# Two-layer hybrid scan and MLP backbone: modulation matmuls in halves of eight, their raw tiles in the ring of the weight halves, and the scan-state update as a sum and a scaling

## The chip, the core and the metric

The kernel runs on one core of a Trainium2 chip. The metric is the device time of one execution in microseconds (us). Inputs and result are fp32: a dense product is made of three single-pass products of split operands, the small products of the scans run in fp32 or, inside a triangular inverse, in fp16.

## The reference, cut to what matters

Two layers over 512 latent and 256 context tokens of width 1024. Each layer has a token mixer (a projection to 44 tiles of 128 columns, four pairs of RWKV-7 heads and two pairs of GLA heads that scan the tokens in both directions, gates, an output projection) and an MLP. Both are modulated by a product of the conditioning vectors with `ada_w`:

```python
mod_lat = (jax.nn.silu(c) @ ada_w[l] + ada_b[l])[:, None, :]
mod_ctx = jax.nn.silu(c_ctx) @ ada_w[l] + ada_b[l]
...
s = s * w_t - (s . kk_t) (kk_t * a_t) + v_t k_t      # RWKV-7 state, per token
...
s_next = s * dec + kv                                 # GLA state, per chunk of 64
```

The kernel computes both scans by chunks of 64 tokens: within a chunk everything is matrix products, and between chunks a state of 64 rows per head is carried on by a multiplication with the chunk's decay E and an addition of what the chunk brings.

## The kernel before, in words

**Stages.** A head part (load, first norm, first third of the modulation), then `mixer(0)`, `out_mlp(0)`, `mixer(1)`, `out_mlp(1)` (L1935 to L2003). In a mixer, 18 units follow each other: four RWKV pairs and two GLA pairs, three groups of 256 tokens each. `rw_C` (L1324) is the serial part of an RWKV unit: four steps `st`, each with both directions `d` and both heads `h` of a pair. A step goes through the engines in this order: TensorE makes `pp` from the state `zs` (in the profile `c<-ZS,AR`), ScalarE and VectorE each copy half of it to `pre`, TensorE makes `pq` (`c<-pre,YI`), both copy it to `za` (`ZA<-c`), TensorE makes `pr` (`c<-ZA,TK`), and the next state is written (`ZS<-c,E,zse`). Before, that last part is two operations: ScalarE scales the old state by E into `zse` (four instructions of 64x64), and VectorE multiplies `pr` by E and adds `zse` (four `scalar_tensor_tensor`). `gla_C` (L1579) does the same with `ze` and `GZ` and instructions of 64x128.

**What lies around the scans.** The dense products of the projections and of the gates (`d<-sh,wh`, `d<-sl,wh`, `d<-sh,wl`) are poured between the scan steps. `ada_steps` (L746) computes the remaining five sixths of the modulation: 5 blocks of 32 steps, each step one DMA of a raw tile `wa` (256 KB), four matmuls with 32 columns of weights (`da<-wa,SC`; the array is used as four column groups), and one addition of 128x128 to `acc` on VectorE; at the end of a block `acc` is transposed by four matmuls with the identity (`da<-C,acc`). The same way of transposing, `mm(..., ident)`, stands in `rstd_b` (L808, `d<-C,sc`) and in `sum_sq` (L815, `d<-C,rn`). Transposes of the scan operands are `pe.transpose` already (`m<-C,BK`).

**Buffers.** A dense weight tile comes in two halves. `load_w` (L674) loads each into a raw tile `wr0` or `wr1` (2 buffers each), ScalarE rounds it to `wh`, and VectorE or GpSimd subtracts to get `wl`. In a mixer the gates and every second output tile use `wr1`, the other projections `wr0`. The raw modulation tile `wa` has a buffer of its own (1).

**Order.** All instructions are recorded by a planner, the class `Order` (L151), and issued in the order of its list schedule, one flush per stage (five). It groups neighbouring matmuls of one kind (L277), gives each node a cost, and picks per engine the earliest ready node; among equals the one due first. `SEG` (L142) holds its settings per stage: HYST is a penalty for a node that changes the shape of TensorE's array, LATE and LATEF delay dense products and gate products against their due time, WARM says from what activity on it prefers dense products, AHEAD and HOLD bound how early DMAs are issued. `CFG` (L102) says how many gate tiles (`nfill`) and modulation steps (`nada`) are recorded with each unit. TensorE, ScalarE, VectorE, GpSimd and the DMA queue of SyncE each work strictly in the issued order. Line 566, where the nodes are issued, is the line of nearly every instruction of the profile, so rows are told apart by their tiles.

Of the kernel before, what the change touches and what calls it, by code (L numbers as in the profile page):

```python
# [53 lines left out]
def constants():  # L54
# [45 lines left out]
SB = 6  # L100

CFG = {  # L102
    "nfill": ((2, 2, 0, 3, 1, 0, 3, 1, 0, 2, 2, 0, 2, 1, 1, 0, 0, 0, 0), (2, 3, 0, 2, 2, 1, 2, 2, 0, 2, 0, 0, 2, 1, 1, 0, 0, 0, 0)),
    "nada": ((2, 2, 2, 2, 2, 2, 2, 2, 2, 1, 2, 2, 0, 1, 0, 0, 0, 0, 0), (2, 1, 3, 1, 3, 2, 3, 1, 0, 0, 0, 0, 0, 0, 0, 0, 0, 0, 0)),
# [38 lines left out]
    dict(AHEAD=20.0, HOLD=8000.0, HYST=0.0, LATE=80000.0, LATEF=80000.0, SLACK=0.0, WARM=0.45),  # L143
    dict(AHEAD=100.0, HOLD=1000000000.0, HYST=0.0, LATE=20000.0, LATEF=20000.0, SLACK=0.0, WARM=0.45),
    dict(AHEAD=20.0, HOLD=1000000000.0, HYST=0.0, LATE=20000.0, LATEF=20000.0, SLACK=0.0, WARM=0.45),
    dict(AHEAD=20.0, HOLD=8000.0, HYST=0.0, LATE=20000.0, LATEF=20000.0, SLACK=0.0, WARM=0.45),
    dict(AHEAD=20.0, HOLD=1000000000.0, HYST=0.0, LATE=20000.0, LATEF=20000.0, SLACK=0.0, WARM=0.6),
# [3 lines left out]
class Order:  # L151
# [57 lines left out]
    def add(self, key, op, fn, a, k):  # L209
# [36 lines left out]
        else:  # L246
            c = max(w(out), max([w(x) for x in ins if x.ap and len(x.ap) > 1], default=0))
            onchip = [x for x in ins if hasattr(x.tensor, "cap_key")]
            if key == "ACT":
                n["d"] = 175.0 + 0.87 * c + (100.0 if any(isinstance(k.get(x), bass.AP) for x in ("bias", "scale")) and c > 64 else 0.0)  # L250
                n["table"] = 1 if k.get("func") == AF.Ln else 0 if k.get("func") in (AF.Exp, AF.Tanh) else None
            elif key == "POOL":
# [4 lines left out]
                elif k.get("op") == ALU.pow:  # L257
                    n["d"] = 380.0 + 160.0 * c
                else:
                    n["d"] = 185.0 + 2.16 * c  # L260
                n["two"] = op == "tensor_tensor"
            else:
# [6 lines left out]
                else:  # L269
                    n["d"] = 150.0 + 1.05 * c  # L270
        if key == "PE":
# [5 lines left out]
            if GROUP and p is not None and p.get("kind") == n["kind"] and p["calls"] < (3 if lhs.dtype == F32R else 4 if n["dense"] else 16):  # L277
# [51 lines left out]
    def flush(self):  # L329
# [6 lines left out]
        for n in ns:  # L336
# [6 lines left out]
            for name, t in ts.items():  # L343
                left[name] = left.get(name, 0) + 1
                if name not in self.serial:
                    key = t.cap_key
                    kk = self.slots.setdefault(key, {"cap": t.bufs or t.tag_meta.bufs, "free": [], "used": 0, "next": {}, "n": {}, "t0": self.free0})
                    sub = "da" if name.startswith("da_") else ""
# [225 lines left out]
def hybrid_kernel(ctx: ExitStack, tc: tile.TileContext, A: dict, out: bass.AP):  # L574
# [171 lines left out]
    def ada_steps(l, b0, pl, tag, bufs):  # L746
        acc = prm.tile([P, 512], F32, name="acc", tag="acc", bufs=1)
        for k in range(KT):
            for u in range(4):
                raw = pl.tile([P, 4, 128], F32, name="wa", tag=tag, bufs=bufs)  # L750
                sp.dma_start(out=raw, in_=A["ada"][l, b0 // 2, k, u].rearrange("p (g m) -> p g m", g=4))
                ps = ips.tile([P, 512], F32, name="da", tag="i")[:, 0:128]
                for g in range(4):
                    mm(ps[32 * g:32 * g + 32, :], SC[:, k, :], raw[:, g])
# [1320 lines left out]
```

## Time and profile before

| | us |
|---|---|
| median of 3 runs | 2871.23 |
| lowest, highest | 2870.66, 2878.29 |
| the profiled execution | 2886.5 |
| its span, first to last instruction | 2884.7 |

| engine | busy us | share of the span |
|---|---|---|
| TensorE, matmuls (PE) | 2714.0 | 94% |
| TensorE, weight loads (PEld) | 2249.0 | 78% |
| VectorE (DVE) | 1603.8 | 56% |
| ScalarE (ACT) | 1470.5 | 51% |
| GpSimd (POOL) | 1172.0 | 41% |

Matmuls overlap each other, so the time that one costs is read from start to start, and a busy share of PE near 100% still hides short gaps. An fp32 matmul has two records, a single-pass one and a transpose have one. The granted clock is a mean over a stretch of TensorE's two levels, 2.4 GHz (1.00) and 1.2 GHz (0.50).

### The profile page before, as it was taken

Reading aid. Unit: us, or ns where it says so; the run is one execution under the profiler, and the core shown is the slowest. Engines: PE = TensorE matmul, PEld = TensorE weight load, DVE = VectorE, ACT = ScalarE, POOL = GpSimd, SP = SyncE. Lnnn points to the kernel's source line nnn. Section 1 sums busy time; section 2 is a strip of 40 time slices with the busy share of each in tenths; the row PEclk is TensorE's granted clock in tenths of the full one; section 3 lists DMA queues with packets and bytes.
Section 4 is the critical chain, followed back from the end, with each engine's and each line's share of the span. In section 5 each row is a group of like instructions: output and inputs, shape, how many; then the busy total and the mean of one; then the engine's idle time right before and its main releaser. Section 6 shows DMA issues by size and latency. Waiting matters only on the chain.

```text
span 2884.7 us, 57083 instructions
## 1 busy us (share of the span) xinstructions
PE 2714.0 (94%) x22596; PEld 2249.0 (78%) x22596; DVE 1603.8 (56%) x3154; ACT 1470.5 (51%) x3144; POOL 1172.0 (41%) x1336
## 2 busy tenths in 40 slices
PE   7999999999989989999999899989988988999998
PEld 6777877788767878888888666767776766888887
DVE  6677787775576351122224547787877677622224
ACT  4565655666773452313134545656566785633333
POOL 3653444443321642313135546434434232733335
PEclk9999999999999999999998999999988999999999
DMA  6322333222226322222223342223211125433334
GB/s 232 110 85 73 97 95 97 84 90 65 87 94 229 94 77 63 64 64 64 63 70 116 119 143 87 77 85 90 92 34 35 34 77 182 136 106 97 97 95 136
DMA packets 148444, 276.59 MB, mean 96 GB/s; under 512 B 16496, under 2 KB 25456, under 8 KB 148176
## 3 DMA queue, kind: packets, MB, share of 16 engines
q1 hardware_dynamic: 148176, 272.93, 30.4%
q8 instruction: 178, 2.92, 0.4%
q14 instruction: 90, 0.74, 0.1%
HBM read 242.85 MB, written 30.02 MB: 95 GB/s over the span
## 4 chain that ended last, share of the span: by engine, by line
PE 51%; DVE 7%; ACT 4%; POOL 4%; issue 2%; DMA 1%; SPq 0%; POOLq 0%; ACTq 0%; DVEq 0%
PE d L566 43%; PE c L566 3%; PE m L566 2%; PE i L566 2%; POOL wl L566 1%; POOL S L566 1%; POOL x L566 1%; DVE sl L566 1%; DVE ZS L566 1%; DVE AR L566 1%; DVE u L566 1%; ACT zse L566 1%; PE da L566 1%; DVE GZ L566 0%; ACT f L566 0%
## 5 line engine op out<-in xcount | busy, mean ns | idle before, releaser
L566 PE MATMUL d<-sh,wh 128*128 128x512 f32 (+1 forms) x3280 | 1199.2, 366 | 39.0 <-ACT sh L566 13.2
L566 PE MATMUL d<-sh,wl 128*128 128x512 f32 (+1 forms) x3280 | 1142.4, 348 | 19.1 <-POOL wl L566 16.4
L566 PE MATMUL d<-sl,wh 128*128 128x512 f32 (+1 forms) x3280 | 1142.1, 348 | 4.4 <-DVE sl L566 3.0
L566 POOL TENSOR_TENSOR wl<-wr,wh 128x512 fp32r<-128x512 f32 x356 | 476.0, 1339 | 793.9 <-ACT wh L566 770.6
L566 PEld LDWEIGHTS d<-sh,wh 128*128 128x128 f32 x3280 | 631.3, 192 | 150.0 <-issue 36.5
L566 PEld LDWEIGHTS d<-sh,wl 128*128 128x128 f32 x3280 | 631.0, 192 | 103.8 <-POOL wl L566 21.9
L566 PEld LDWEIGHTS d<-sl,wh 128*128 128x128 f32 x3280 | 632.7, 193 | 69.0 <-DVE sl L566 5.4
L566 ACT ACTIVATE wh<-wr 128x512 fp32r<-128x512 f32 x580 | 361.9, 627 | 469.3 <-PE d L566 389.6
L566 DVE TENSOR_TENSOR wl<-wr,wh 128x512 fp32r<-128x512 f32 x224 | 171.5, 770 | 187.0 <-ACT wh L566 178.9
L566 DVE TENSOR_TENSOR t<-t,d 128x512 f32<-128x512 f32 (+1 forms) x101 | 58.2, 576 | 318.2 <-ACT t L566 318.1
L566 POOL TENSOR_TENSOR sl<-t,sh 128x512 fp32r<-128x512 f32 (+2 forms) x72 | 103.3, 1435 | 204.8 <-ACT sh L566 204.7
L566 DVE TENSOR_TENSOR a<-a,d 128x512 f32<-128x512 f32 (+1 forms) x80 | 44.3, 554 | 232.7 <-PE d L566 232.7
L566 ACT ACTIVATE zse<-ZS,E 64x64 f32<-64x64 f32 x352 | 121.3, 345 | 67.2 <-DVE ZS L566 62.7
L566 ACT ACTIVATE XY<-i 128x512 f16<-128x512 f32 x192 | 107.8, 591 | 59.1 <-PE i L566 57.1
L566 ACT ACTIVATE t<-d 128x512 f32<-128x512 f32 (+1 forms) x101 | 51.4, 509 | 161.4 <-PE d L566 161.3
L566 DVE SCALAR_TENSOR_TENSOR ZS<-c,E,zse 64x64 f32<-64x64 f32 x352 | 99.5, 283 | 34.6 <-PE c L566 27.6
L566 POOL TENSOR_TENSOR LTL<-AB,LTB 64x512 f16<-64x512 f32 x48 | 63.9, 1332 | 122.1 <-DVE LTB L566 88.1
L566 POOL TENSOR_TENSOR rn<-rn,C 128x2 f32<-128x2 f32 (+2 forms) x41 | 59.3, 1446 | 101.4 <-DVE rn L566 94.9
L566 POOL TENSOR_TENSOR S<-S,q 128x256 f32<-128x256 f32 x92 | 76.5, 838 | 56.5 <-ACT q L566 52.8
L566 PEld LDWEIGHTS <-XY 64*64 64x64 f16 x1920 | 65.7, 110 | 38.9 <-issue 27.2
L566 DVE TENSOR_TENSOR Q<-i,MK 128x512 f16<-128x512 f32 x120 | 82.7, 689 | 23.3 <-PE i L566 20.7
L566 ACT ACTIVATE f<-d 128x512 f32<-128x512 f32 (+1 forms) x85 | 54.0, 644 | 79.1 <-PE d L566 69.2
(255 smaller groups left out, 4309.6 us busy)
## 6 DMA issues: line engine op xcount, KB each, us to landing
wr<-in_w_dram SPq DMA_DIRECT2D x304, 256.0 KB, 2.6
wr<-in_win_dram SPq DMA_DIRECT2D x180, 256.0 KB, 2.9
wa<-in_ada_dram SPq DMA_DIRECT2D x160, 256.0 KB, 2.7
wr<-in_wmrg_dram SPq DMA_DIRECT2D x64, 256.0 KB, 2.9
ra<-in_ada_dram SPq DMA_DIRECT2D x32, 256.0 KB, 5.4
wr<-in_wout_dram SPq DMA_DIRECT2D x32, 256.0 KB, 3.0
gdr<-fg SPq DMA_DIRECT2D x20, 384.0 KB, 2.9
gdr<-fg SPq DMA_DIRECT2D x20, 256.0 KB, 2.3
```

The lines of the kernel that those rows point to most:

```text
L566: ins = fn(*a, **k).ins
```

## The change

1. **Modulation in halves.** A step of `ada_steps` takes two raw tiles, issues eight matmuls into 128x256 of PSUM and adds 128x256 to `acc`: 16 steps a block in place of 32. The planner may group 8 such matmuls (before: 4).
2. **Raw tiles in the ring `wr1`.** `wa` has no buffer of its own any more; it shares `wr1`, which gets 3 buffers (before: 2, and 1 for `wa`).
3. **Transposes.** `mm(..., ident)` becomes `pe.transpose(..., ident)` at four places: 88 calls in `rstd_b`, 42 in `sum_sq`, 24 at the ends of the modulation blocks.
4. **Update as sum and scaling.** No `zse` and no `ze`. In layer one (`ACCUM[0]` is False) VectorE adds `pr` and the old state into `gs`, then multiplies by E: two instructions for each of two heads, both directions in one. In layer two (`ACCUM[1]`) TensorE adds the old state in PSUM by a matmul with the identity ahead of the one with `tk`, and VectorE multiplies by E: one instruction for each head. `gla_C` adds and multiplies on VectorE in both layers.
5. **Planner.** Some costs, the settings of all five stages and the tables `nfill` and `nada`.

```diff
+ACCUM = (False, True)
...
-    dict(AHEAD=20.0, HOLD=8000.0, HYST=0.0, LATE=80000.0, LATEF=80000.0, SLACK=0.0, WARM=0.45),
-    dict(AHEAD=100.0, HOLD=1000000000.0, HYST=0.0, LATE=20000.0, LATEF=20000.0, SLACK=0.0, WARM=0.45),
...
-    dict(AHEAD=20.0, HOLD=8000.0, HYST=0.0, LATE=20000.0, LATEF=20000.0, SLACK=0.0, WARM=0.45),
...
+    dict(AHEAD=20.0, HOLD=8000.0, HYST=2000.0, LATE=80000.0, LATEF=80000.0, SLACK=0.0, WARM=0.42),
+    dict(AHEAD=20.0, HOLD=1000000000.0, HYST=2000.0, LATE=20000.0, LATEF=20000.0, SLACK=0.0, WARM=0.4),
...
+    dict(AHEAD=400.0, HOLD=1000000000.0, HYST=0.0, LATE=20000.0, LATEF=0.0, SLACK=0.0, WARM=0.3),
...
-            raw = wp.tile([P, 4, 128], F32, name="wr", tag=f"wr{i}", bufs=2)
+            raw = wp.tile([P, 4, 128], F32, name="wr", tag=f"wr{i}", bufs=2 + i)
...
-                for g in range(4):
-                    mm(ps[32 * g:32 * g + 32, :], SC[:, k, :], raw[:, g])
-                au = acc[:, 128 * u:128 * u + 128]
+                for v in range(2):
+                    for g in range(4):
+                        mm(ps[32 * g:32 * g + 32, 128 * v:128 * v + 128], SC[:, k, :], raws[v][:, g])
+                au = acc[:, 256 * u:256 * u + 256]
...
-            mm(pt[:, s].rearrange("p g r -> p (g r)"), acc[:, 128 * s:128 * s + 128], ident)
+            pe.transpose(pt[:, s].rearrange("p g r -> p (g r)"), acc[:, 128 * s:128 * s + 128], ident)
...
-                if not (gi == NG - 1 and st == 3):
-                    zse = G([P, 2, 64], "zse", 1)
-                    for d in range(2):
-                        for h in range(2):
-                            act.activation(out=zse[HS[h], d], in_=zs[HS[h], cc[d], h, :], func=AF.Copy, scale=E[HS[h], cc[d]:cc[d] + 1])
...
                 for d in range(2):
-                    mm(fl(pr[:, d]), tk[:, cc[d]], fl(za[:, cc[d]]))
-                for d in range(2):
-                    for h in range(2):
-                        hs = HS[h]
-                        dve.scalar_tensor_tensor(out=nz[hs, ns[d], h, :], in0=pr[hs, d, h], scalar=E[hs, cc[d]:cc[d] + 1],
-                                                 in1=zse[hs, d], op0=ALU.mult, op1=ALU.add)
+                    if ACCUM[l]:
+                        mm(fl(pr[:, d]), ident, fl(zs[:, cc[d]]), stop=False)
+                    mm(fl(pr[:, d]), tk[:, cc[d]], fl(za[:, cc[d]]), start=not ACCUM[l])
+                for h in range(2):
+                    hs = HS[h]
+                    src = pr[hs, :, h]
+                    if not ACCUM[l]:
+                        src = G([P, 2, 64], "gs", 1)[hs]
+                        dve.tensor_tensor(out=src, in0=pr[hs, :, h], in1=zs[hs, sl, h, :], op=ALU.add)
+                    dve.tensor_tensor(out=nz[hs, ns, h, :], in0=src, in1=E[hs, sl].unsqueeze(2).to_broadcast([64, 2, 64]), op=ALU.mult)
...
-            g = ada_steps(l, b0, wp, "wa", 1)
-            r += [("a", g)] * (4 * KT)
+            g = ada_steps(l, b0, wp, "wr1", 3)
+            r += [("a", g)] * (2 * KT)
```

**How the order moves.** First TensorE in the second mixer, around the end of a scan step. `c` is the PSUM tile of the scan, `ZA` and `TK` the operands of `pr`, `ZS` the old state, `C` the constants (here the identity), `da<-wa,SC` the modulation. Before:

```order
L566 MATMUL d<-sh,wh 128x512
L566 MATMUL d<-sl,wh 128x512
L566 MATMUL d<-sh,wl 128x512
L566 MATMUL c<-pre,YI 128x64 x2
L566 MATMUL da<-wa,SC 32x128 x4
L566 MATMUL d<-C,sc 128x2 x4
L566 MATMUL c<-ZA,TK 128x128 x2
```

With the change:

```order
L567 MATMUL d<-C,sc 128x2 x6
L567 MATMUL c<-pre,YI 128x64 x2
L567 MATMUL da<-wa,SC 32x128 x8
L567 MATMUL c<-ZS,C 128x128
L567 MATMUL c<-ZA,TK 128x128
L567 MATMUL c<-ZS,C 128x128
L567 MATMUL c<-ZA,TK 128x128
L567 MATMUL d<-sh,wh 128x512
L567 MATMUL d<-sl,wh 128x512
L567 MATMUL d<-sh,wl 128x512
```

The modulation stands in runs of eight (79 runs in the whole program, before 158 of four), and the matmul with the identity stands directly ahead of the one that waits for `ZA`, behind everything that `ZA` is made from.

Second, VectorE in the first mixer at the update of the state (`XY` and `Q` belong to the triangular inverse of the unit behind, `lw` and `ta` to the decays). Before:

```order
L566 COPY ZA<-c 64x2x64
L566 SCALAR_TENSOR_TENSOR v<-sc,PH,v 128x512
L566 SCALAR_TENSOR_TENSOR ZS<-c,E,zse 64x64 x4
L566 TENSOR_TENSOR AB<-m,MK 64x512 x2
L566 TENSOR_TENSOR acc<-acc,da 128x128
L566 TENSOR_TENSOR AR<-m,MK 64x4x128 x2
L566 COPY pre<-c 64x128
```

With the change:

```order
L567 COPY ZA<-c 64x2x64
L567 TENSOR_TENSOR LTB<-AB,MK 64x8x64
L567 TENSOR_TENSOR gs<-c,ZS 64x128
L567 TENSOR_TENSOR ZS<-gs,E 64x2x64
L567 TENSOR_TENSOR XY<-i,MK 128x8x64
L567 TENSOR_TENSOR gs<-c,ZS 64x128
L567 TENSOR_TENSOR ZS<-gs,E 64x2x64
L567 SCALAR_TENSOR_TENSOR ta<-ta,kk 128x256
L567 COPY pre<-c 64x128
```

The sum and the scaling of one head stand together; `gs` has one buffer, and in 38 of the 44 steps of the first layer another instruction stands between the two heads. In the second layer the two scalings stand together (`ZS<-c,E 64x2x64 x2`).

Third, the DMA queue of SyncE in the first mixer. Before:

```order
L566 DMA wr<-in_win_dram 128x512
L566 DMA wa<-in_ada_dram 128x512 x3
L566 DMA wr<-in_win_dram 128x512
L566 DMA gdr_89<-fg 128x768
L566 DMA wr<-in_win_dram 128x512
L566 DMA wa<-in_ada_dram 128x512 x4
L566 DMA wr<-in_win_dram 128x512
```

With the change:

```order
L567 DMA gdr_89<-fg 128x768
L567 DMA wa<-in_ada_dram 128x512
L567 DMA wr<-in_win_dram 128x512 x2
L567 DMA wa<-in_ada_dram 128x512 x5
L567 DMA wr<-in_win_dram 128x512 x2
L567 DMA wa<-in_ada_dram 128x512
L567 DMA wr<-in_win_dram 128x512 x2
```

The number of DMAs is the same; raw modulation tiles and raw weight halves still alternate in one queue, now also in one ring where the halves are those of a gate.

## Rows read from the trace of the kernel before

**Rows 1.** The page, busy time of TensorE and its granted clock in 40 slices.
```profile
PE   7999999999989989999999899989988988999998
...
PEclk9999999999999999999998999999988999999999
```
**Rows 2.** Windows: us; busy PE, PEld, DVE, ACT, POOL (count); PEclk; DMA share; GB/s.
```profile
70.00:650.00 580.00, 568.23 (x6679) 458.53 (x6679) 435.13 (x906) 341.21 (x812) 273.61 (x345) 1.00 0.30 91
650.00:885.00 235.00, 217.57 (x1807) 178.86 (x1806) 154.36 (x317) 157.99 (x319) 64.15 (x97) 0.97 0.27 85
885.00:1620.00 735.00, 705.35 (x3924) 616.59 (x3924) 235.17 (x414) 249.83 (x475) 263.94 (x228) 0.97 0.29 90
...
1700.00:2230.00 530.00, 492.23 (x5629) 388.08 (x5627) 404.68 (x838) 318.32 (x751) 248.06 (x300) 0.93 0.26 78
2230.00:2420.00 190.00, 158.28 (x1275) 126.06 (x1272) 132.66 (x269) 140.95 (x299) 50.89 (x89) 0.92 0.21 63
```
**Rows 3.** Chain that ended last, shares of the stretch: 1700 to 2230, then 2230 to 2420.
```profile
by line: PE d L566 27.5%; PE c L566 15.3%; PE m L566 8.9%; PE i L566 8.2%; issue 3.8%; DVE AR L566 3.6%; DVE ZS L566 3.5%; ACT zse L566 3.1%; PE da L566 2.8%; DVE AB L566 2.0%; DVE ZA L566 2.0%; DVE BK L566 1.5%; DVE YI L566 1.0%; DVE Q L56
by line: PE d L566 20.3%; issue 15.8%; PE c L566 7.7%; DVE GZ L566 7.0%; PE m L566 4.9%; DVE lw L566 4.9%; DVE QS L566 4.3%; DVE sc L566 3.9%; ACT L566 3.4%; ACT ta L566 2.5%; ACT ze L566 2.1%; ACT f L566 1.8%; ACT GZ L566 1.7%; ACT sc L566
```
**Rows 4.** Timeline of PE in the first mixer: start us, us, operation, xcount.
```profile
312.29 0.61 PE L566 MATMUL c<-AB,ZA 128*128 128x128 f32 x4
312.74 1.50 PE L566 MATMUL d<-C,sc 128*128 128x128 f32 x12
314.17 0.43 PE L566 MATMUL da<-wa,SC 128*32 128x128 f32 x8
314.53 0.50 PE L566 MATMUL d<-sh,wh 128*128 128x512 f32 x1
314.86 0.40 PE L566 MATMUL d<-sl,wh 128*128 128x512 f32 x1
315.10 0.39 PE L566 MATMUL d<-sh,wl 128*128 128x512 f32 x1
```
**Rows 5.** The same view: four transposes, then what starts behind them.
```profile
487.38 0.63 PE L566 MATMUL m<-C,BK 128*128 128x128 f32 x4
487.84 1.06 PE L566 MATMUL da<-C,acc 128*128 128x128 f32 x8
```
**Rows 6.** Timeline of a scan step in the second mixer (in brackets the engine's idle time).
```profile
2040.04 0.82 PE L566 MATMUL c<-ZS,AR 128*128 128x128 f32 x4
2040.41 1.46 ACT L566 ACTIVATE zse<-ZS,E 64x64 f32<-64x64 f32 x4 [4.76 <-DVE ZS L566]
...
2041.90 0.27 ACT L566 ACTIVATE pre<-c 64x128 f32<-64x128 f32 x1
...
2042.22 0.66 PE L566 MATMUL c<-pre,YI 128*128 128x64 f32 x4 [0.36 <-ACT pre L566]
```
**Rows 7.** Groups by shape: xcount | busy us, mean ns | idle before, releasers.
```profile
L566 ACT ACTIVATE zse<-ZS,E 64x64 f32<-64x64 f32 x352 | 121.3, 345 | 67.2 <-DVE ZS L566 62.7
L566 DVE SCALAR_TENSOR_TENSOR ZS<-c,E,zse 64x64 f32<-64x64 f32 x352 | 99.5, 283 | 34.6 <-PE c L566 27.6
L566 DVE SCALAR_TENSOR_TENSOR GZ<-c,E,ze 64x128 f32<-64x128 f32 x176 | 61.5, 349 | 10.6 <-PE c L566 5.1 <-ACT ze L566 0.4
L566 DVE TENSOR_TENSOR t<-t,d 128x256 f32<-128x256 f32 x42 | 17.6, 420 | 27.1 <-ACT t L566 27.0
L566 DVE TENSOR_TENSOR AR<-r,lw 64x256 f32<-64x256 f32 x40 | 19.9, 498 | 0.2
```
**Rows 8.** Waits of the DMA queue, 70 to 650: us in total, times, longest.
```profile
SPq L566 <- PE da L566: 187.9, 69, 14.1
```
**Rows 9.** The page, weight halves: splitting on POOL and ACT, and landing (last column us).
```profile
L566 POOL TENSOR_TENSOR wl<-wr,wh 128x512 fp32r<-128x512 f32 x356 | 476.0, 1339 | 793.9 <-ACT wh L566 770.6
...
L566 ACT ACTIVATE wh<-wr 128x512 fp32r<-128x512 f32 x580 | 361.9, 627 | 469.3 <-PE d L566 389.6
...
wr<-in_win_dram SPq DMA_DIRECT2D x180, 256.0 KB, 2.9
```

More of the change, by code (lines that the diff above doesn't have):

```diff
@@ L249, in add @@
             if key == "ACT":
-                n["d"] = 175.0 + 0.87 * c + (100.0 if any(isinstance(k.get(x), bass.AP) for x in ("bias", "scale")) and c > 64 else 0.0)
+                n["d"] = 175.0 + 0.87 * c + (110.0 if any(isinstance(k.get(x), bass.AP) for x in ("bias", "scale")) and c > 32 else 0.0)
                 n["table"] = 1 if k.get("func") == AF.Ln else 0 if k.get("func") in (AF.Exp, AF.Tanh) else None
@@ L269, in add @@
                 else:
-                    n["d"] = 150.0 + 1.05 * c
+                    n["d"] = 150.0 + 1.05 * c + (60.0 if op == "scalar_tensor_tensor" and isinstance(k.get("scalar"), bass.AP) else 0.0)
         if key == "PE":
@@ L276, in add @@
             p = self.nodes[-1] if self.nodes else None
-            if GROUP and p is not None and p.get("kind") == n["kind"] and p["calls"] < (3 if lhs.dtype == F32R else 4 if n["dense"] else 16):
+            if GROUP and p is not None and p.get("kind") == n["kind"] and p["calls"] < (3 if lhs.dtype == F32R else 8 if n["dense"] else 16):
                 p["call"].append((fn, a, k))
@@ L748, in ada_steps @@
         for k in range(KT):
[L749 to L752, printed above, removed]
-                for g in range(4):
-                    mm(ps[32 * g:32 * g + 32, :], SC[:, k, :], raw[:, g])
-                au = acc[:, 128 * u:128 * u + 128]
+            for u in range(2):
+                ps = ips.tile([P, 512], F32, name="da", tag="i")[:, 0:256]
+                raws = []
+                for v in range(2):
+                    raw = pl.tile([P, 4, 128], F32, name="wa", tag=tag, bufs=bufs)
+                    sp.dma_start(out=raw, in_=A["ada"][l, b0 // 2, k, 2 * u + v].rearrange("p (g m) -> p g m", g=4))
+                    raws.append(raw)
+                for v in range(2):
+                    for g in range(4):
+                        mm(ps[32 * g:32 * g + 32, 128 * v:128 * v + 128], SC[:, k, :], raws[v][:, g])
+                au = acc[:, 256 * u:256 * u + 256]
                 if k == 0:
@@ L1673, in ada_one @@
             next(g)
-            yield 2 * 512
+            yield 4 * 512
         def run(g):
@@ L1722, in mixer @@
             f = [fills.pop(0) for _ in range(min(nfill[w + 1], len(fills)))]
-            a = [adas.pop(0) for _ in range(min(4 * nada[w + 1], len(adas)))]
-            dc[w] += fill_c * len(f) + 1024 * len(a)
+            a = [adas.pop(0) for _ in range(min(2 * nada[w + 1], len(adas)))]
+            dc[w] += fill_c * len(f) + 2048 * len(a)
             if i == 5:
@@ L1963, in hybrid_kernel @@
             pt = cps.tile([P, 4, 4, 32], F32, name="da", tag="c")[:, 0]
-            mm(pt.rearrange("p g r -> p (g r)"), au, ident)
+            pe.transpose(pt.rearrange("p g r -> p (g r)"), au, ident)
             dve.tensor_tensor(
```

40 lines of the change are left out of this document (19 added, 21 removed).

## The prediction

> **What bounds the kernel now.** I read first the busy slices of the page [rows 1]: TensorE shows nine tenths or more in nearly all of them, and the granted clock dips in a few. A busy matmul row still hides gaps, so the second view is the windows by stage [rows 2]. They give three kinds of stretch. The RWKV part of the first mixer (70 to 650) has TensorE busy 568.2 of 580 us at a clock of 1.00: it is bound by TensorE's own work, and a microsecond less of that work is nearly a microsecond less of time. The first MLP with its surroundings (885 to 1620) is close to that: 705.4 of 735 us. The RWKV part of the second mixer (1700 to 2230) is different: TensorE is busy 492.2 of 530 us, so it idles 38 us, and the clock averages 0.93. With two levels, 14% of the stretch, some 74 us, ran at the lower one. The GLA part behind it (2230 to 2420) idles 32 of 190 us at 0.92. The second mixer has 512 columns where the first has 768 in its gates, so it has less dense work to pour between the scan steps.
>
> The third view is the chain that ended last in the second mixer (first line of [rows 3]): the PE shares listed (d, c, m, i, da) make 62.7%, but the state update (`ZS`) is on it with 3.5% and ScalarE's `zse` with 3.1%. The fourth is one step in time [rows 6]: TensorE starts `c<-ZS,AR` at 2040.04, the `zse` group holds ScalarE from 2040.41 to 2041.87, ScalarE's half of `pre` starts at 2041.90, and only then `c<-pre,YI` starts. So `zse`, which reads the same new state, stands in the queue ahead of the copy that the next matmul waits for. That is what the removal of `zse` is worth: not 121 us of ScalarE [rows 7], but the place that it takes on the chain.
>
> **Prices on TensorE.** From start to start, four fp32 records take 0.45 us (312.29 to 312.74 in [rows 4]), 0.111 each, and an fp32 call has two: 0.222. Four transposes take 0.46 us [rows 5], 0.115 each, one record a call. A call that becomes a transpose saves about 0.11. Twelve records should take 1.34 us, but the modulation behind them starts after 1.43 (312.74 to 314.17 in [rows 4]): 0.09 for the change of the array's shape. The first dense matmul behind other work takes 0.33 to the next start, the second 0.24 [rows 4]: 0.09 for starting a dense run again.
>
> **The change part by part.** (1) Runs of eight: counted over the whole order, changes of shape fall from 544 to 477 in the first mixer, from 16 to 6 in the MLP behind it, from 475 to 419 in the second mixer; that includes what the new penalty for such changes does. At 0.09 these are 6.0, 0.9 and 5.0 us. Starts of dense runs fall by 17, 6 and 9: 1.5, 0.5 and 0.8 us. The number of modulation matmuls stays. Their additions halve in number; a pair of about 0.28 us each (the nearest is `ZS` in [rows 7]) becomes one of 0.42 (the 128x256 addition from PSUM [rows 7]), off the path, with TensorE's work as its cover; without that cover it is still a gain.
>
> (2) Transposes: 60 calls in the first mixer (48 and 12), 24 in the first MLP, 48 in the second mixer (40 and 8), 12 in the last MLP, at 0.11: 6.6, 2.6, 5.3 and 1.3 us. The 10 in the head part count nothing, loads cover them there. The Trainium skill ("TensorE: Matmul & The Clock Gate", Terms) says that transpose mode is four times faster for FP32. Rows 4 and 5 show twice, 0.222 against 0.115; by the Trainium skill's factor the 144 calls would save 24 us in place of 15.8 and the sum below would be 8 us lower. The measured rows decide.
>
> (3) The update, layer one: four instructions of 0.283 us [rows 7] become two sums and two scalings of 64x128, which no row has; by width they lie between the 64x64 update (0.283) and the 64x256 product of two on-chip operands (0.498) [rows 7], and I take 0.283 for each, being the nearest in width and fixed cost. That is 1.13 us as before. But `gs` has one buffer, and in 38 of 44 steps another VectorE instruction stands between the heads, so the second head's state is later by up to half a microsecond; the first head's is earlier, and `zse` is gone from ahead of `pre`. In a stretch with TensorE 98% busy I cost both at nothing; if that cover were thinner, 38 times 0.5 = 19 us would be the most that it costs.
>
> (4) The update, layer two: one scaling per head, so of the 18.6 us that `ZS` has on the chain (3.5% of 530) half goes, 9.3 us, and `zse` leaves with 16.4 us (3.1%). Against that come 88 identity matmuls of 0.222: 19.5 us of TensorE's time. They stand directly ahead of the matmul that waits for `ZA`, so I count them in full. With (1) and (2), TensorE in this mixer gets 19.5 - 5.0 - 0.8 - 5.3 = 8.4 us more work. On the chain the sum is 8.4 - 9.3 - 16.4 = -17.3 us. A removed piece uncovers the next: TensorE's waits for `AR`, `AB` and `pre` are close by. I take half, -9. The bounds are +8.4 (nothing of the chain comes out) and -17.3 with part of the lower clock won back besides.
>
> (5) GLA: per layer 88 updates of 0.349 us become 44 sums of 0.42 and 44 scalings between 0.42 and 0.50 [rows 7], 37 to 40 us for 31. `GZ` has 7.0% of 190 us on the chain (second line of [rows 3]), 13.3 us, which grow by some 3 to 4; `ze` leaves with 2.1%, 4.0 us. Nothing in sum.
>
> (6) The ring: the same number of DMAs and of buffers, shared. Nothing, as long as a gate's weights are split well before their matmuls; priced below.
>
> **The sum.** First mixer 6.0 + 1.5 + 6.6 = 14.1; of it I count 13.5, since its GLA part is not full. First MLP 0.9 + 0.5 + 2.6 = 4.0, counted 3.5; last MLP 1; second mixer 9; GLA nothing. Together -27 us. The profiled execution took 2886.5, of which 2884.7 are its span; it would take 2859. It stands 15 us above the median of the three runs shown, so on that scale I expect 2871.2 - 27 = **2844**. From no change, 0.3% (8.6 us) is about what can be told here.
>
> **The rivals.** *The chain opens.* The second mixer is held by the chain, not by TensorE: all -17.3 us come out, the pauses shorten, and two thirds of what the lower clock costs there come back. The two stretches ran 74 + 30 us at half speed, which cost 52; two thirds are 35. With 18 from the rest: 2871 - 17 - 35 - 18 = **2801**. For it: rows 6. Against it: the planner's new settings keep long runs of TensorE's order without a dense matmul in the second mixer (the longest 462 calls before, 281 now, but more middling ones). Chance 0.18.
>
> *The identity eats it.* TensorE holds the second mixer after all: +8.4 there, and the torn updates of layer one cost half of their 19 us; -18 elsewhere: **2871**, no change (2863 to 2880). For it: the 62.7% of PE on the chain. Against it: 38 us of idle. That single-record transposes do not come out faster than rows 5 say, or that the regrouping is lost in other reordering, ends here too. Chance 0.15.
>
> *The ring starves the gates* (slower). In the first mixer the DMA queue already stands 187.9 us behind the modulation matmuls [rows 8]; now two raw modulation tiles may hold two of three buffers of the gates' ring, and a gate half loaded too late exposes its landing (2.9 us), rounding (0.63) and subtraction (1.34) [rows 9], 4.9 us. There are 80 gate halves. From 6 exposed ones on the gain is gone, from 8 on the kernel is measurably slower; 12 give 2844 + 58 = **2902**. Against it: raw buffers are as many as before, and the rounded halves have two more behind them. Chance 0.10.
>
> *The clock stays down* (slower). With transposes and identity work in place of dense work nearby, TensorE falls to the lower level more often. Each microsecond there costs half of one: 54 us more of it undo the forecast gain, from 71 us on the kernel is measurably slower, and 80 us over both mixers give 2844 + 40 = **2884**. Against it: 70 to 650 ran at 1.00 [rows 2] with transposes like those of rows 5 throughout. The Trainium skill ("TensorE: Matmul & The Clock Gate", Part 4) says that transpose mode does not count as busy for the clock in the way other matmuls do; by that rule the 108 new transposes of the mixers would push this way, and in the first mixer the trace does not show it. Chance 0.07.
>
> **How the numbers follow.** The forecast (about 2826 to 2862) has 0.50. Faster is the forecast and the opened chain, 0.68; the same, 0.15; slower, the two last, 0.17. The range from 2796 to 2886 takes in most of the opened chain and the bounds of part (4), and leaves out some 0.05 below and 0.12 above.
>
> **What would show it.** In the profile of the changed kernel: `d<-C,sc` 128x128, `d<-C,rn` and `da<-C,acc` with half their records; runs of 16 records of `da<-wa,SC`, the dense row behind them no later than before; 70 to 885 shorter by 13 to 14 us; in the second mixer ScalarE's `pre` free right behind `c<-ZS,AR`, idle time of TensorE below 38 us, and a clock no lower than 0.93. The forecast is wrong if PE's waits for `wl` in the mixers come to more than 20 us, if the clock in 1700 to 2230 falls, or if the MLPs change by more than 5 us, where nothing but transposes and order is touched.

## The result, and the profile after

The changed kernel takes **2811.44 us** (median of 4 runs, 2808.33 to 2814.92) beside 2874.55 for the kernel before (4 runs); the ratio is **0.978, 95% interval 0.976 to 0.980**. The forecast was 2844: the sign was right and the time lies in the range, but the gain is 63 us where 27 were expected. The profiled execution took 2812.3 us, its span 2810.5.

The page, busy slices and granted clock of the changed kernel, which answer to [rows 1]:

```profile
PE   7999999999989999999999899999989979899998
...
PEclk9999999999999989999999899999999999999999
```

To compare stages, both kernels are cut at the same events: first and last `c<-ZS,AR` of each layer and last write of `GZ`. Windows of the kernel before (us; busy PE, PEld, DVE, ACT, POOL with counts; granted clock; DMA share; GB/s): RWKV part and GLA part of the first mixer, first MLP with its surroundings, RWKV part and GLA part of the second mixer, the rest.

```profile
123.80:692.00 568.20, 557.36 (x6669) 451.11 (x6666) 425.20 (x914) 338.72 (x806) 246.65 (x314) 1.00 0.28 86
692.00:871.70 179.70, 164.78 (x1327) 134.44 (x1326) 117.91 (x239) 129.62 (x259) 52.07 (x78) 0.96 0.27 86
871.70:1745.80 874.10, 839.24 (x4745) 717.32 (x4745) 303.87 (x521) 316.11 (x594) 335.60 (x324) 0.97 0.31 97
1745.80:2268.40 522.60, 481.78 (x5636) 382.38 (x5635) 404.92 (x853) 322.33 (x771) 226.51 (x289) 0.92 0.23 68
2268.40:2407.50 139.10, 117.31 (x907) 90.93 (x906) 98.82 (x200) 107.40 (x222) 37.01 (x61) 0.93 0.22 66
2407.50:2884.70 477.20, 448.42 (x2441) 387.42 (x2440) 175.30 (x291) 194.93 (x366) 211.65 (x186) 0.97 0.40 124
```

The same windows of the changed kernel (lengths less busy PE are TensorE's idle time):

```profile
122.90:674.80 551.90, 541.51 (x6638) 447.50 (x6637) 444.85 (x884) 279.40 (x628) 246.95 (x314) 1.00 0.29 90
674.80:854.90 180.10, 166.06 (x1290) 136.24 (x1290) 132.64 (x233) 96.83 (x172) 55.12 (x77) 0.95 0.26 84
854.90:1725.00 870.10, 840.64 (x4806) 718.52 (x4805) 306.89 (x518) 316.05 (x595) 338.61 (x329) 0.97 0.31 99
1725.00:2204.00 479.00, 451.94 (x5674) 371.13 (x5669) 382.13 (x738) 261.14 (x588) 221.68 (x283) 0.98 0.23 70
2204.00:2334.60 130.60, 108.82 (x887) 85.08 (x886) 104.67 (x196) 74.18 (x138) 40.53 (x61) 0.96 0.20 61
2334.60:2810.50 475.90, 449.87 (x2461) 387.07 (x2459) 177.16 (x294) 194.25 (x366) 214.06 (x186) 0.98 0.41 127
```

| stage | forecast us | measured us |
|---|---|---|
| first mixer (both parts) | -13.5 | -15.9 |
| first MLP | -3.5 | -4.0 |
| second mixer, RWKV part | -9 | -43.6 |
| second mixer, GLA part | 0 | -8.5 |
| the rest | -1 | -1.3 |

Nearly all of the surplus lies in the second mixer. In its RWKV part TensorE's idle time fell from 40.8 to 27.1 us, and the granted clock rose from 0.92 to 0.98: by its two levels that is 84 us at 1.2 GHz before (0.08 x 2 x 522.6) and 19 after, so up to 32 of the 43.6 us, half of the difference, are clock. (The profiled run of before, with a clock of 0.967 against 0.970 in the mean of its later runs, is 12 us longer than the median; the stages add up to 74 us less where the medians differ by 63.)

On the chain of that stretch, in place of the first line of [rows 3], `zse` is gone and `ZS` fell from 3.5 to 1.1%:

```profile
by line: PE d L567 33.4%; PE c L567 20.8%; PE i L567 12.4%; PE m L567 10.4%; PE da L567 2.3%; issue 1.6%; DVE lw L567 1.5%; DVE ZS L567 1.1%; DVE AR L567 1.1%; DVE ZA L567 1.0%; ACT XY L567 0.9%; DVE YI L567 0.9%; DVE AB L567 0.8%; DVE XO L
```

What the new update costs, groups by shape that answer to [rows 7] (count, then busy us and mean ns of one, then idle time before it):

```profile
L567 DVE TENSOR_TENSOR ZS<-gs,E 64x128 f32<-64x128 f32 x88 | 43.8, 498 | 3.0
L567 DVE TENSOR_TENSOR GZ<-gs,E 64x256 f32<-64x256 f32 x88 | 43.1, 490 | 2.8
L567 DVE TENSOR_TENSOR gs<-c,GZ 64x256 f32<-64x256 f32 x88 | 37.0, 420 | 12.5 <-PE c L567 11.2
L567 DVE TENSOR_TENSOR acc<-acc,da 128x256 f32<-128x256 f32 x70 | 28.8, 416 | 11.2 <-PE da L567 10.4
L567 DVE TENSOR_TENSOR gs<-c,ZS 64x128 f32<-64x128 f32 x88 | 25.3, 288 | 16.9 <-PE c L567 14.9
L567 DVE TENSOR_TENSOR ZS<-c,E 64x128 f32<-64x128 f32 x88 | 25.3, 287 | 14.1 <-PE c L567 12.7
```

And the end of a scan step in layer two, TensorE's timeline. The modulation's 16 records take 0.57 us (1908.89 to 1909.46, 0.036 each), and the first identity matmul (`c<-ZS,C`) runs while `ZA` is being copied, the second does not:

```profile
1908.30 0.66 PE L567 MATMUL c<-pre,YI 128*128 128x64 f32 x4 [0.19 <-DVE YI L567]
1908.89 0.64 PE L567 MATMUL da<-wa,SC 128*32 128x128 f32 x16
1909.46 0.49 PE L567 MATMUL c<-ZS,C 128*128 128x128 f32 x2
1910.16 0.49 PE L567 MATMUL c<-ZA,TK 128*128 128x128 f32 x2 [0.21 <-ACT ZA L567]
1910.48 0.39 PE L567 MATMUL c<-ZS,C 128*128 128x128 f32 x2
1910.71 0.39 PE L567 MATMUL c<-ZA,TK 128*128 128x128 f32 x2
```

The DMA queue in the first mixer's RWKV part, waits in us, times, longest: before (one line, beside [rows 8]), then changed:

```profile
SPq L566 <- POOL wl L566: 91.6, 42, 7.5
```

```profile
SPq L567 <- POOL wl L567: 189.5, 39, 23.5
SPq L567 <- PE da L567: 154.0, 41, 12.4
```

The queue does stand longer behind the splitting of weights with the shared ring, but TensorE waited for a `wl` once in the first mixer (2.0 us) and never in the second.

### The profile page after: what moved, and what is told of

Its sections match the earlier page's. It is cut to its first block, busy times and chain, and to the rows that moved or that the text cites. A ratio compares the mean times of both kernels' runs of the same rounds, so it can differ in the third digit from the quotient of the medians.

```text
span 2810.5 us, 56340 instructions
## 1 busy us (share of the span) xinstructions
PE 2662.9 (95%) x22618; PEld 2229.4 (79%) x22618; DVE 1624.6 (58%) x2996; ACT 1282.8 (46%) x2606; POOL 1179.3 (42%) x1336
## 4 chain that ended last, share of the span: by engine, by line
PE 76%; DVE 9%; POOL 4%; ACT 4%; DMA 4%; issue 3%; SPq 0%; POOLq 0%; ACTq 0%; DVEq 0%
PE d L567 58%; PE c L567 8%; PE m L567 5%; PE i L567 4%; PE da L567 1%; POOL wl L567 1%; DVE lw L567 1%; DVE ZA L567 1%; POOL S L567 1%; POOL x L567 1%; DMA ra<-in_ada_dram 1%; DVE ZS L567 1%; ACT f L567 1%; DMA wr<-in_win_dram 1%; DVE sc L567 1%
## 5 line engine op out<-in xcount | busy, mean ns | idle before, releaser
L567 PE MATMUL d<-sh,wh 128*128 128x512 f32 (+1 forms) x3280 | 1192.0, 363 | 28.1 <-ACT f L567 10.8
L567 DVE TENSOR_TENSOR Q<-i,MK 128x512 f16<-128x512 f32 x120 | 82.7, 689 | 18.3 <-PE i L567 15.5
L567 PE MATMUL i<-Q,XY 64*64 64x64 f16 x1920 | 80.5, 197 | 7.9 <-DVE Q L567 5.0
L567 PEld LDWEIGHTS <-LTB 128*128 128x128 f16 x1344 | 60.3, 99 | 26.9 <-issue 21.1
```

What stands on the lines that cost most here:

```text
L567: ins = fn(*a, **k).ins
```

## The experiments

Three theories. **A**: `zse` cost its place on the chain, and its removal opened the second mixer. **B**: the new tables and settings made the gain. **C**: TensorE's own work (transposes, runs of eight) made it. Every edit makes the planner write a new order, so some kernels were changed only where instructions are issued (in `Order.issue`, behind the planning): their order is that of their parent, instruction by instruction.

One figure is used beside the times. Each run's time multiplied by its mean granted clock is what it would take if the time at 1.2 GHz ran twice as fast; I call it *time at full clock*, and the remainder what the lower clock costs at most. Means over the runs:

| kernel | median us | ratio to before (95%) | at full clock | remainder |
|---|---|---|---|---|
| before | 2875 to 2880 | 1 | 2790 | 84 to 90 |
| e1 `zse` behind `pre`, fixed order | 2918.0 | 1.012 to 1.017 | 2815 | 101 |
| e2, e10 update alone, two plans | 2873.9, 2883.4 | 0.998 to 1.001, 1.001 to 1.003 | 2790, 2797 | 83, 87 |
| e7, e11 modulation and transposes alone, two plans | 2874.5, 2886.3 | 0.998 to 1.001, 1.001 to 1.004 | 2774, 2769 | 100, 118 |
| e18 update and transposes | 2867.3 | 0.994 to 0.997 | 2783 | 86 |
| e4, e12 all edits, old settings, two plans | 2835.5, 2850.5 | 0.984 to 0.988, 0.989 to 0.992 | 2762, 2762 | 74, 88 |
| e3 changed, update undone | 2862.9 | 0.994 to 0.997 | 2754 | 109 |
| changed | 2811.4 | 0.976 to 0.980 | 2749 | 63 |
| e5 changed, transposes as matmuls, fixed order | 2824.1 | 0.980 to 0.985 | 2763 | 63 |
| e6 changed, identity left out, fixed order | 2809.1 | 0.974 to 0.979 | 2736 | 74 |
| e13 e3 with useless matmuls, fixed order | 2865.4 | 0.995 to 0.998 | 2775 | 92 |
| e14 changed, useless matmuls in layer one, fixed order | 2826.9 | 0.980 to 0.985 | 2764 | 62 |
| e15 changed, pauses filled, fixed order | 2827.7 | 0.981 to 0.985 | 2792 | 36 |
| e17 changed, MLP pauses filled, fixed order | 2816.2 | 0.976 to 0.979 | 2770 | 46 |
| e8 changed, planner cost off by 1 ns | 2833.4 | 0.983 to 0.987 | 2756 | 78 |
| e9 before, planner cost off by 1 ns | 2882.6 | 1.000 to 1.002 | 2791 | 92 |
| e16 new settings alone | 2889.3 | 1.003 to 1.007 | 2796 | 95 |

**Which part makes the gain.** The first four kernels.

```diff
# e1, in Order.issue of the kernel before: each zse node is held back until pre is issued on ScalarE
+            if n["eng"] == "ACT" and wrote(n, "zse_"):
+                hold.append(n)
+                continue
...
# e2: before, with ACCUM and the new rw_C and gla_C. e3: changed, with the old ones.
# e4: changed, with nfill, nada, SEG and the costs of before
```

> The kernel before with its order unchanged on every engine but ScalarE, where zse is issued behind the copy pre of the same step in place of ahead of it. Theory A (zse cost its place on the chain): the second mixer's scans get 8 to 17 us shorter and the time falls to 2855 to 2864 us; the first mixer, full on TensorE, moves by less than 3. Theory B (the new tables and planner settings made the gain): 2868 to 2876 us, nothing moves. Theory C (TensorE's own work, transposes and runs of eight, made it): the same, 2868 to 2876.

> The kernel before with the new update alone (zse and ze gone, sum and scaling, layer two in PSUM); tables, settings, modulation and transposes as before. Theory A: most of the gain of the second mixer is here, with part of the lower clock won back: 2825 to 2850 us. Theory B: 2865 to 2885, since the old tables still leave long stretches without dense work. Theory C: 2871 to 2891, as 20 us of identity matmuls are added to a full TensorE.

> The changed kernel with the update of the kernel before (zse and ze back, both layers); all else as changed. Theory A: 2835 to 2860 us, the second mixer 25 to 45 us longer. Theory B: 2805 to 2820, the second mixer as in the changed kernel. Theory C: 2790 to 2812, as the identity matmuls are gone.

> The changed kernel with the tables (gates and modulation per unit), the stage settings and the costs of the planner as before; the work of every engine is that of the changed kernel. Theory A: 2811 to 2828 us. Theory B: 2845 to 2870, with 50 to 80 us of the second mixer at the lower clock again. Theory C: 2811 to 2820.

e1 came out 43 us slower than before, which none of the theories had. ScalarE's timeline of a step in its second mixer shows why (the matmul `c<-ZS,AR` began at 2032.69, `c<-pre,YI` at 2033.98):

```profile
2033.33 0.27 ACT L578 ACTIVATE pre<-c 64x128 f32<-64x128 f32 x1 [0.77 <-PE c L578]
2033.51 0.69 ACT L578 ACTIVATE zse<-ZS,E 64x64 f32<-64x64 f32 x2
2034.22 1.08 ACT L578 ACTIVATE XY<-i 128x512 f16<-128x512 f32 x2
2035.19 0.26 ACT L578 ACTIVATE ZA<-c 64x128 f32<-64x128 f32 x1
```

`pre` is early, but `zse` now pushes `XY` and the copy of `ZA`. In the mean over the 48 steps of each mixer, ScalarE's half of `pre` starts 0.46 and 0.41 us earlier behind the last `c<-ZS,AR`, and ScalarE's half of `ZA` 0.3 and 0.5 us later behind its matmul. VectorE's half of `pre`, the later of the two in 61 of the 96 steps, stays where it was in the mean (2.8 and 2.5 us behind), and so does the matmul that needs both: `c<-pre,YI` begins 5.41 and 5.42 us behind the end of the last `c<-ZS,AR` before, 5.47 and 5.40 in e1. So on the whole `zse` did not hold the chain at `pre`. And the first mixer, where TensorE is 98% busy, lost 20.7 us by it (568.2 to 588.9, at a clock of 0.99), its idle time going from 10.8 to 22.5 us: here a busy TensorE did not hide a delay on ScalarE. The window of e1:

```profile
123.10:712.00 588.90, 566.35 (x6669) 458.23 (x6666) 428.12 (x914) 336.03 (x808) 244.60 (x314) 0.99 0.27 83
```

e2 is worth nothing, e3 loses 51 of the 63 us, e4 keeps 39 of them. e4 lies in none of the ranges, e3 just above that of A. So neither A nor B nor C alone: the update is worth much beside the other edits and nothing without them. (e3 is one new plan under the new settings; e8, below, is another with the update in it, at 2833.4. Against that one e3 loses 30 us, so some 20 of the 51 can be the plan.)

**Prices in a fixed order, and the planner's luck.**

```diff
# e5, in Order.issue of the changed kernel, for the four transposes of fp32 tiles "d.."
-                ins = fn(*a, **k).ins
+                if n["eng"] == "PE" and n["kind"][2] == "transpose" and a[0].tensor.name.startswith("d"):
+                    ins = self.tc.nc.tensor.matmul(a[0], lhsT=a[1], rhs=a[2], start=True, stop=True).ins
...
# e6: the matmul with lhsT=ident is not issued, the one behind it gets start=True
# e7: before, with the new ada_steps, ring, grouping and pe.transpose
# e8: changed, with
-                    n["d"] = 215.0 + 2.25 * c
+                    n["d"] = 214.0 + 2.25 * c
```

> The changed kernel with its order unchanged on every engine; only the transposes at the four places are issued as matmuls with the identity again. If each lies on TensorE's path at 0.11 us, as the prediction counts them: 144 times 0.11 = 15.8 us more, about 2827 us. If TensorE's waits cover half of those in the mixers: 2820. If they are covered altogether, or if the matmuls keep the clock up: 2811 to 2815.

> The changed kernel with its order unchanged, but the 88 identity matmuls of layer two are left out, so the old state is missing from the sum in layer two. If TensorE's work holds the second mixer, as term (4) of the prediction counts it: 19.5 us less, about 2792 us. If the identity matmul runs while TensorE would wait for ZA anyway: 2808 to 2812. Between them the share of the waits: 2800.

> The kernel before with the modulation in halves, its ring, the runs of eight and the transposes; update, tables and settings as before. By the prediction's terms (1) and (2), without the second mixer's loss to the identity: 30 us less, 2840 to 2848. If the update gives nothing under the old plan in this setting either (as in the run with the update alone): like the run with the plan undone, 2833 to 2838. If the update gives its gain only beside these edits: 2850 to 2865.

> The changed kernel with one planner cost off by 1 ns (fixed cost of a GpSimd operation, 214 in place of 215); no work changes, only what the list schedule makes of near ties. It measures what an arbitrary new plan costs beside the one that the settings were chosen for. If plans are smooth: 2808 to 2815. If the settings were fitted to one plan: 2820 to 2840, and differences of that size between the other runs are then no property of an edit.

e5 took 2824.1 us (five runs, 2819.6 to 2834.9): the transposes are worth 12.7 us, 14.0 at full clock, with the same mean clock (0.9776 and 0.9778). e8 took 2833.4: a new plan by 1 ns of one cost is 22 us slower, which speaks for settings fitted to one plan, though only one neighbour was tried. e6 took 2809.1, 2.4 us less than the changed kernel and inside the spread of both: 88 matmuls less are worth next to nothing. Its second mixer, RWKV part:

```profile
1723.00:2202.40 479.40, 448.24 (x5496) 362.69 (x5492) 381.43 (x738) 260.58 (x588) 221.63 (x284) 0.94 0.22 70
```

The stretch is as long as with them (479.0), but its clock is 0.94 in place of 0.98. One profile of an unchanged stretch moves by some us: in e14 and e17, below, whose second mixer is issued in the changed kernel's order, it lasted 481.1 and 483.2 us, both at 0.97; neither fell to 0.94:

```profile
1732.10:2213.20 481.10, 454.13 (x5672) 373.52 (x5668) 381.13 (x738) 260.69 (x587) 222.03 (x284) 0.97 0.22 70
1720.40:2203.60 483.20, 455.81 (x5672) 375.06 (x5668) 382.01 (x738) 260.33 (x587) 222.13 (x285) 0.97 0.22 70
```

At full clock it is 451 against 469 us, so 19 us less work, as 88 x 0.222 says; and the lower clock takes about as much back. Over the runs it is 13 us of work less and 11 of remainder more. Waits for `ZA` that would have covered the identity matmuls explain little of it: without them TensorE's idle time grew by 4.1 us (27.1 to 31.2).

e7 took 2874.5, slower than all three ranges: it saves 16 us at full clock, and the clock takes back about as much. Four more plans, with the cost of e8 off by 1 ns (184 for 185 in the old settings), measure how much of this is luck of the plan:

> The kernel before with one planner cost off by 1 ns (184 in place of 185 for a GpSimd operation). If the settings of the kernel before were fitted to its plan as those of the changed one were: 2885 to 2905 us, and the edits tried alone, at 2874, were gains of 10 to 30 against an arbitrary plan. If the plan of before was an ordinary one: 2865 to 2882.

> The kernel with the update alone, planned again with the same cost off by 1 ns. If a plan's luck is about 20 us wide and the update by itself is worth something like 20: anything from 2840 to 2880, mean with the first plan below that of the two plans of before by 10 to 25. If the update is worth nothing without the other edits: the mean of the two equals that of the two plans of before within 10.

> The kernel with the modulation and transposes alone, planned again with the same cost off by 1 ns. With the transposes at 13 us by the run that undid them in an unchanged order, and the runs of eight at some 10: mean of the two plans 15 to 25 below that of the two plans of before. If these edits only lower TensorE's work and its clock takes it back: the same mean within 10, with more time at the lower clock.

> All edits with the old tables, settings and costs, planned again with the same cost off by 1 ns. If the 39 us of the first such plan are a property of the edits: 2825 to 2845. If that plan was a lucky one: 2850 to 2865, and the edits are worth some 15 to 30 us on an arbitrary plan, near the 27 forecast.

Under the old settings two plans of one kernel differ by 3 to 12 us (by their ratios), and the means of the pairs stand at 1.0005 (before), 1.001 (update), 1.001 (modulation and transposes) and 0.988 (all edits): nothing, nothing, and 36 us. The remainder column shows the larger part of this. With modulation and transposes alone the work at full clock falls by 16 to 21 us and the remainder rises by some 20; with the update beside them the work falls by 28 and the remainder is no higher than before.

**Is it the clock?** Useless matmuls (identity times identity, overwritten at once) in a fixed order, where the clock is low, where it is full, and in pauses.

```diff
# e13 (on e3, second mixer) and e14 (on the changed kernel, first mixer), ahead of each matmul with TK and ZA
+                    todo.insert(0, (fn, a, dict(k, lhsT=self.ident, rhs=self.ident)))
# e15: int((pause - 150) / 222) of them in each planned pause over 0.9 us, into the next product's tile
# e16: before, with nfill, nada, SEG and the costs of the changed kernel
```

> The kernel with the update undone, in unchanged order, plus 88 useless matmuls in layer two: identity times identity, written where the matmul with TK directly behind overwrites it, two a step. If the identity matmuls keep TensorE's clock up (theory of the clock): the added 18 us of work cost less than 6, as time at the lower clock falls; 2855 to 2869 us against 2862.9. If work on a chain is simply work: 2875 to 2884.

> The changed kernel, in unchanged order, plus the same 88 useless matmuls in layer one, whose scans ran at a granted clock of 1.00, so that no lower clock can be won back. Theory of the clock: the full 88 times 0.222 = 19.5 us, 2826 to 2833. If TensorE's waits for ZA cover such matmuls in either layer: 2811 to 2818.

> The changed kernel, in unchanged order, with useless identity matmuls in TensorE's longer planned pauses (over 0.9 us, behind the head part), 220 in 33 places, written where the next product overwrites them. Theory of the clock: some of the 60 us that the lower clock costs come back, above all around the norms of the MLPs, 2790 to 2806. If pauses do not set the clock, or if the useless matmuls delay what comes behind them: 2811 to 2825.

> The kernel before with the new tables, stage settings and costs of the planner alone; update, modulation and transposes as before. If the settings are good for any kernel: 2845 to 2860. If they pay only with the edits that they were chosen for: 2868 to 2890.

e13 took 2865.4, 2.5 us more than e3; e14 2826.9, 15.5 more than the changed kernel. The second mixer of e3, then of e13:

```profile
1724.50:2235.10 510.60, 460.80 (x5476) 370.35 (x5473) 397.69 (x819) 316.30 (x754) 217.45 (x275) 0.91 0.21 65
```

```profile
1719.30:2240.00 520.70, 470.32 (x5653) 384.04 (x5650) 398.32 (x818) 316.05 (x754) 216.80 (x273) 0.93 0.20 64
```

and the first mixer of e14, to be held against 551.9 us at 1.00:

```profile
123.40:691.90 568.50, 560.39 (x6816) 469.03 (x6814) 442.57 (x884) 278.50 (x627) 245.64 (x314) 1.00 0.28 88
```

Where the clock is full the 88 matmuls lengthen the stretch by 16.6 us. In the second mixer the profiled stretch grew by 10.1 us, at a clock of 0.93 for 0.91; over the runs of e13 the remainder falls from 109 to 92 while the work at full clock rises by 21, and the kernel is 2.5 us longer. So the clock gave back between half of them and nearly all, as the theory of the clock asked for; plain work would have cost the same in both. Nor did they run in waits that were there anyway: TensorE's idle time in the second mixer is 49.8 us in e3 and 50.4 in e13.

e15 raised the clock from 0.978 to 0.987 and was 16 us slower, above both ranges. Its trace shows fillings that ran behind the pause, not in it: they waited for VectorE's `u`, that is, for the tile that they write (13 records from 989.25 on after 3.17 us of waiting, 13 from 1565.19 on after 5.90). e16 made before 0.5% slower: the new settings help only together with the other edits. Two last kernels:

```diff
# e17: as e15, in the two MLP stages alone, into a PSUM buffer that is idle there
+            od.spare = cps.tile([P, 512], F32, name="spare", tag="c")[:, 0:128]
# e18: before, with the new update and pe.transpose
```

> The changed kernel, in unchanged order, with 142 useless identity matmuls in the planned pauses (over 0.9 us) of the two MLP stages alone, written into a PSUM buffer that nothing else uses there, so that they run in the pause and not behind it as those of the run with all pauses filled did. Theory of the clock: the lower clock cost 29 and 11 us in the two stages; half to two thirds of the first come back, 2788 to 2801. If the matmuls cost what they win: 2808 to 2815. If they delay what follows: 2815 to 2830.

> The kernel before with the update and the transposes; modulation, its ring, tables and settings as before. All edits under the old settings gave 0.986 and 0.990 of before. If the transposes are what joins with the update: 0.987 to 0.993, 2841 to 2858. If the modulation in halves and its runs of eight are: 0.995 to 1.001, 2864 to 2881.

e17 took 2816.2, a ratio of 0.9776 (0.976 to 0.979), the same as the changed kernel's. The first MLP:

```profile
853.90:1720.40 866.50, 848.69 (x5019) 729.98 (x5018) 307.25 (x518) 315.68 (x595) 337.31 (x327) 0.99 0.31 100
```

The clock there is 0.99 for 0.97, so 35 us less at 1.2 GHz, and the stage is 3.6 us shorter; the last stage got 5 us longer. The trace has 106 of the useless matmuls in this stage, 23.5 us of work at 0.222; TensorE's idle time fell by 11.7 us (29.5 to 17.8), so only half of them ran in pauses, and the other half used up most of the 17 us that the clock can give back. (The 3.6 us are no more than noise: in e14 the same stage, untouched, lasted 862.7.) So filled pauses do raise the clock, but no version faster than the changed kernel came of it. e18 gave 0.9956: of the 36 us of all edits, update and transposes together bring some 14 in this one plan, and the rest comes with the modulation in halves beside them.

## Why the prediction was right, and where it failed

**Parts (1) and (2), TensorE's work: right in sum, in part by luck.** First mixer 15.9 us for 13.5, MLPs 4.0 and 1.3 for 3.5 and 1. But with the old settings the same edits shorten the first mixer by 8 and 6 us (traces of e4 and e12), and the new settings alone by 6 (e16), so its 15.9 us hold a share of the settings, for which the sum had no term. The transposes measured 12.7 us by e5 for 15.8. They start 0.109 us apart in the changed kernel (six in a row at 84.75), as [rows 5] had it, and their records halved as foretold. The Trainium skill's factor of four for FP32 ("TensorE: Matmul & The Clock Gate", Terms) would by estimate have made them worth 24; no run here shows it. The modulation in halves, with its grouping, is worth 16 and 27 us by e18 against e12 and e4, for 14.7 forecast (its 6.0, 0.9, 5.0, 1.5, 0.5 and 0.8); these are different plans, so the size is loose.

**Part (3), layer one: right, on a wrong ground.** The sum took 0.288 as assumed, the scaling 0.498 in place of 0.283, and the second mixer's scaling from PSUM 0.287. But "In a stretch with TensorE 98% busy I cost both at nothing" gives no good reason: in e1 a delay in that stretch cost 20.7 us. The stretch gained 16.3 us all the same, in another order; what the update alone did there no run separates.

**Part (4), layer two: failed; here the forecast went wrong.** The sum was "half goes, 9.3 us, and `zse` leaves with 16.4 us", against it 88 identity matmuls that count "in full" with 19.5 us, and of the result "I take half, -9". Measured: 43.6 us less in the RWKV part. The step that failed is that this sum has no term for the granted clock, though the prediction itself read 74 us at the lower level from [rows 2]; it left them to a bound and to a rival. At full clock the stretch went from 481 to 469 us (0.92 x 522.6, 0.98 x 479.0), 11 us less and near the 9 forecast; the other 32 are the 65 us fewer at 1.2 GHz. The settings are only part of it: under the old ones the stretch lasts 493.9 and 501.2 us at 0.97 and 0.96 (e4, e12), against 522.6 and 518.1 at 0.92 and 0.94 (before, e9). That is 23 us less on average, of which up to 19 are clock (38 us less at 1.2 GHz). The stretch in e9, e4 and e12:

```profile
1753.70:2271.80 518.10, 473.16 (x5633) 372.04 (x5632) 399.11 (x852) 322.81 (x771) 223.61 (x287) 0.94 0.23 69
1731.50:2225.40 493.90, 462.29 (x5730) 378.79 (x5725) 378.70 (x740) 261.49 (x588) 226.72 (x288) 0.97 0.23 72
1736.70:2237.90 501.20, 466.16 (x5716) 379.34 (x5711) 381.02 (x740) 259.99 (x589) 226.53 (x286) 0.96 0.23 71
```

For the same reason the price of the identity matmuls fell. They are 19 us of work at full clock, as counted, but leaving them out won 2.4 us and no length of the stretch (e6): they hold the clock up and so pay for most of themselves (e13 the same with useless ones; e14, where the clock is full, the contrary). That `zse` held the chain at `pre`, read from one step in [rows 6], is not borne out either: e1 put `pre` ahead and lost 43 us, and the update without the other edits gave nothing (e2, e10).

**Parts (5) and (6).** The GLA updates cost what was forecast (sum 0.420, scaling 0.490) and the part still gained 8.5 us, its clock going from 0.93 to 0.96. That gain belongs to the plan: in e8, the same work in another plan, the part lasted 140.6 us at 0.90. The ring did nothing to TensorE that its waits show (2.0 us for a `wl`).

**What no term had.** Under the old settings all edits are worth 36 us, against 27 forecast. The other 29 us, from a mean ratio of 0.988 to 0.978, came with the new tables and settings, of which a change of one cost by 1 ns takes 22 away. The prediction counted what the new order does to shapes of the array, but had no term for the plan itself, which moves the time in ways that such counts don't show.

**The rivals.** The one that came nearest is *the chain opens* (2801): its 35 us of clock are what the windows show (84 + 19 us at 1.2 GHz before, 19 + 10 after, half of the difference 37). Its evidence against, long runs without dense matmuls, pointed the other way: the longest stretch between two dense matmuls of the second mixer fell from 63 us (from 2122 on) to 35 (from 2090 on). It had a chance of 0.18. But its time came out near by luck in part: its 17 us of chain were not shown, and the settings were not in it. *The identity eats it* counted work that the clock gave back. *The ring starves the gates*: waits for `wl` of 2 us against the 20 named. *The clock stays down* did not happen in the changed kernel, but it did in e7 and e11, where modulation and transposes came without the update. The Trainium skill ("TensorE: Matmul & The Clock Gate", Part 4) says that full clock does not engage for transposes, which do not count as busy in the same way. e5 exchanged 154 of them for matmuls in the order of the changed kernel, and the mean clock did not move (0.9778 and 0.9776); whether they lower it in e7 and e11 no run here shows.

**What stays open.** Why the update cures the clock that the other edits lower is shown only in part: the identity work is one reason, worth 11 us of remainder over the runs of e6, and the shorter step may be another, which was not tried alone. What the new settings do to the order, and how much of their 29 us another plan would keep, is open. Two plans per kernel don't separate effects below some 10 us, and a stage is known from one profile of each kernel.

## What to carry to other kernels

In a stretch with pauses, TensorE's work and its clock have to be summed together: work taken out of it can come back as a lower clock, and work added to it can cost much less than its length, so price an added matmul by the granted clock of its own stretch. A busy share of 98% is no cover by itself: in a fixed order a delay on a helper engine cost 20.7 us there. And where an order is searched for, compare edits over several plans, in length and in clock: here one nanosecond in a cost was worth a third of the whole gain.

## What the runs showed of the hardware that was not expected

The same 88 useless matmuls lengthened a stretch at a clock of 1.00 by 16.6 us and its kernel by 15.5; in a stretch at 0.91, in another kernel, it was 10.1 and 2.5.

Leaving 88 matmuls out of a stretch at 0.98 left its length as it was (479.0 and 479.4 us) and brought its clock to 0.94.

VectorE's scaling of two operands in SBUF is stretched beside GpSimd. VectorE's timeline and then GpSimd's at the end of a unit in layer one:

```profile
672.32 1.32 DVE L567 TENSOR_TENSOR ZS<-gs,E 64x128 f32<-64x128 f32 x1
673.67 0.29 DVE L567 TENSOR_TENSOR gs<-c,ZS 64x128 f32<-64x128 f32 x1
674.00 0.29 DVE L567 TENSOR_TENSOR ZS<-gs,E 64x128 f32<-64x128 f32 x1
```

```profile
672.20 1.30 POOL L567 TENSOR_TENSOR wl<-wr,wh 128x512 fp32r<-128x512 f32 x1 [6.89 <-ACT wh L567]
```

Beside this `wl` the scaling takes 1.32 us and ends 0.14 us behind it; alone it takes 0.29. Of the 88, 37 took over 0.30, and a GpSimd instruction ran beside each of these; one ran beside 17 of the other 51 too, so not every one stretches it. The 88 sums and the 88 scalings of the same 64x128 that read PSUM never took over 0.30, though GpSimd ran beside 54 and 64 of them. The Trainium skill ("VectorE: DVE Perf Modes", Two Vector instructions with no wait between them) says that the second of two SBUF inputs is read through an interface shared with GpSimd, which agrees with this trace. It is one reason to form the sum in PSUM.
